# Moving the fourth RWKV batch behind four query tiles, with small group norm factors and attention second in the output projection

## The chip, the cores and the metric

The kernel runs on one core of one Trainium2 chip. The metric is the device time of one execution in microseconds (us). Engines: TensorE (PE, and PEld for its weight loads), VectorE (DVE), ScalarE (ACT), GpSimd (POOL) and SyncE (SP), which here only issues DMAs. Each engine takes its instructions in the order in which they were built and waits for others by semaphores.

## The reference

One layer of a hybrid decoder, for a prompt of 256 tokens and 8 single decode tokens, together T = 264 columns:

```python
x = x + 0.5 * swiglu(rmsnorm(x, n1), f1g, f1u, f1d)        # 2048 -> 5504 -> 2048
proj = rmsnorm(x, nm) @ w_in                                # 2048 -> 4864
o_att = attend(q, k, v, sinks)                              # 16 query heads, 4 kv heads, window 128
out, shift, S = rwkv_time_mix(...)                          # 16 heads of 64, a matrix state per head
x = x + concatenate([o_att, out]) @ w_out
x = x + 0.5 * swiglu(rmsnorm(x, n2), f2g, f2u, f2d)
y = rmsnorm(x, final_norm)
# in rwkv_time_mix, per head of 64:
mean = y.mean(-1); var = ((y - mean) ** 2).mean(-1)
yn = (y - mean) * rsqrt(var + GN_EPS) * ln_w + ln_b          # the group norm
out = (yn + bonus) * g
```

All numbers are float32, and the states, the key and value windows and the shifted columns are outputs too.

## The kernel before

Activations stand with features on the 128 partitions and the 264 tokens along the row. Every weight product (`gemm`, line 136) splits weights and activations into a high and a low part in float32r and adds three matmuls, hi·hi, hi·lo and lo·hi. A weight chunk (`chunk`, 125) is 128 rows by 4 blocks of 128: SyncE loads it into `raw` (6 buffers, line 131), ScalarE casts it to `hi` (132) and VectorE subtracts to get `lo` (133; 4 buffers each). So a chunk is twelve matmuls of 264 columns, and lines 131 to 133 run ahead of TensorE as far as the buffers allow. Results go to one of three `acc` buffers in PSUM; small products use five buffers named `m`.

Between the two feed-forward parts lies `mixing_body` (357). Its main loop walks `SEQ`, a written-out list: an entry `('b', i)` computes six tiles of `w_in` for two pairs of RWKV heads (batch i), `('kv', i)` one key or value tile, `('q', i)` one query tile. Side work is in generators, `tasks`: after each chunk `tick` (83) takes every task one `yield` further, and `pause(n)` sits out n ticks. `prep` (426) prepares a head pair; `chain` (553) does a batch's triangular solves (`X`, `Xt`, `st`, `PT`, `TT`), the state steps (`W`, `BT`, `N`, `S`) and the group norm (`gnorm`, 707); `attend` (760) handles a query tile and `dec_attend` (820) the decode tokens. After the loop the output projection runs in the three passes of `PASS`, each over some of the 16 input blocks (0 to 7 RWKV, 8 to 15 attention); `drain` first finishes the tasks that a pass needs. A scheduler then sets each engine's final order from modelled durations, with priority for lines 131 to 133.

Names: `pj` is a projected RWKV tile, `shc` its last columns (line 412), stored by ScalarE's DMA `out_sh` (887) once all 24 tiles are there; `o` is a query tile, `kv` a key tile, `y` a head pair's output, `gm` the masked products, `sa` their copy in DRAM, `XD` and `XR` the decode operands as they are and turned (701 to 704), `x` or `x0`, `x1` the residual, `e` and `s`, `dr` (new) a block for split activations, small factors and their copy in DRAM. Helper lines are named in the profile by the helper: 59 is `tt`, 62 `stt`, 69 `act`, 75 `mm`.

Of the kernel before, what the change touches and what calls it, by code (L numbers as in the profile page):

```python
# [24 lines left out]
HALF = (slice(0, 64), slice(64, 128))  # L25
# [5 lines left out]
ROW = 320  # L31
NWARM = 11
NGM, NKR, NUV, NTT, NBT = 10, 5, 3, 2, 5
NSTEP = 4
DWAIT = (11, 11, 11, 3)
PW = (2, 1, 3, 2, 9)
ALPHA = math.exp(-0.5)
LKV = 26
SEQ = [('b', 0), ('b', 1), ('b', 2), ('b', 3), ('kv', 0), ('kv', 1), ('kv', 2), ('kv', 3), ('q', 0), ('q', 1), ('q', 2), ('q', 3), ('q', 4), ('q', 5), ('q', 6), ('q', 7)]
PASS = [[0,1,2,3],[4,5,6,7],[8,9,10,11,12,13,14,15]]  # L40

VG1, VGM, VG2, VGF = 0, 16, 32, 48
VMU, VKK, VKA, VA0, VRK, VLW, VLB, VSK, VSD = 64, 90, 98, 106, 114, 122, 130, 138, 154
NVEC = 155
# [3 lines left out]
def body(tc, I, O):  # L48
    nc = tc.nc
    V, A, G, TE, SP = nc.vector, nc.scalar, nc.gpsimd, nc.tensor, nc.sync  # L50
# [3 lines left out]
    def uid(s):  # L54
        cnt[0] += 1
        return f"{s}{cnt[0]}"

    def tt(e, out, a, b, op):
        return e.tensor_tensor(out=out, in0=a, in1=b, op=op)  # L59
# [8 lines left out]
    def act(out, in_, f, **k):  # L68
        return A.activation(out=out, in_=in_, func=f, **k)  # L69

    def bc(ap, shape):
        return ap.broadcast_to(list(shape))

    def mm(out, lhsT, rhs, start=True, stop=True, **k):
        return TE.matmul(out, lhsT, rhs, start=start, stop=stop, **k)  # L75

    def behind(i):
        tc.add_manual_dep(i.ins, big[0].ins.name, mybir.DependencyInfo(mybir.DependencyClass.NoSync, mybir.DependencyReason.SCHED_ONLY))
        return i

    tasks = []

    def tick(hold=()):
        for g in list(tasks):
            if g not in hold and next(g, tasks) is tasks:
                tasks.remove(g)

# [12 lines left out]
    with ExitStack() as ctx:  # L100
# [56 lines left out]
        eps = cp.tile([P, 2], F32, name="eps")  # L157
# [199 lines left out]
        def mixing_body(mx, n2, n3, XD, XR):  # L357
# [3 lines left out]
            def ring(shape, tag, bufs):  # L361
                return mx.tile(list(shape), F32, tag=tag, bufs=bufs, name=uid(tag))
# [6 lines left out]
            ident, bo, cm = C[:, CID:CID + P], C[:, CBO:CBO + P], C[:, CCM:CCM + P]  # L369
# [50 lines left out]
            class Batch:  # L420
                pass

            def c4(x):
                return x[:, :NP].rearrange("p (c t) -> p c t", c=4)

# [127 lines left out]
            def chain(bt):  # L553
                n = bt.n
# [15 lines left out]
                for s in range(1, 31):  # L570
                    m, w = -(-s // ng), 31 - s
                    t = ring((ng * nr, m, w), "st", 2)
# [3 lines left out]
                    tt(V, Y[:, :m, s + 1:], Y[:, :m, s + 1:], t, ALU.add)  # L576
                    if s % NSTEP == 0:
                        yield
# [7 lines left out]
                for h in range(2):  # L586
                    x = h * 64
                    V.transpose(TT[x:x + 32, :, 0:32], TN[x:x + 32])
                yield from pause(7)
                ps = mp()  # L590
                for k in range(n):
                    for c in range(4):
                        for h in range(2):
                            j = k * 4 + c
# [3 lines left out]
                for h in range(2):  # L598
                    r = slice(h * 64 + 32, h * 64 + 64)
                    A.copy(zs[r], ps[r, :n * P].rearrange("p (c t) -> p c t", t=32))  # L600
                yield
                ps = mp()
                for j in range(4 * n):
                    for h in range(2):
                        r = slice(h * 64 + 32, h * 64 + 64)
                        mm(ps[h * 64:h * 64 + 32, j * 32:j * 32 + 32], zs[r, j, :], TT[r, j, 32:64])
                for h in range(2):
                    r = slice(h * 64, h * 64 + 32)
                    A.copy(TT[r, :, 32:64], ps[r, :n * P].rearrange("p (c t) -> p c t", t=32))
                yield  # L610
                Ys = [yb[bt.p0 + k] for k in range(n)]
                uv = bt.UV
                N = ring((P, n, 4, 64), "N", 1)
# [9 lines left out]
                for k in range(n):  # L623
                    v = wus[k].rearrange("p (c t) -> p c t", c=4)
                    for h in range(2):
                        (V.tensor_copy, A.copy)[h](uv[HALF[h], :, k, HALF[h]], v[HALF[h], :, 64:128])
                yield
                pbs = [mp() for _ in range(n)]
                for k in range(n):
                    for c in range(1, 4):  # L630
                        x = (c - 1) * P
                        for h in range(2):
                            r = HALF[h]
                            mm(pbs[k][r, x:x + 64], W[r, k, c - 1, :], bt.BT[k][r, c, r])
                        for h in range(2):
                            r = HALF[h]
# [23 lines left out]
                for c in range(1, 4):  # L660
                    ps = mp()
                    for k in range(n):
                        for h in range(2):
                            r = HALF[h]
                            mm(ps[r, k * 64:k * 64 + 64], PT[r, k, c - 1, :], S[r, k])
                    for k in range(n):
                        for h in range(2):
                            r = HALF[h]
# [13 lines left out]
                    A.dma_start(O["wkvp"][bt.p0 + k], S[:, k])  # L682
                g2s = [load(I["g2"][bt.p0 + k], (P, P)) for k in range(n)]
                gps = []
                gs = [gnorm(Ys[k]) for k in range(n)]
                for _ in range(PW[3] + 1):
                    for g in gs:
                        next(g)
                    yield
                for k in range(n):  # L690
                    p, o = bt.p0 + k, Ys[k]
# [3 lines left out]
                    stt(o, o, vc(VLB + p), gp[:, :T], ALU.add, ALU.mult)  # L695
                    mixed[p] = o
                if len(bts) == nbat and bt is bts[-1]:
                    ps = mp()
                    xt = mp()
                    for i in range(5):  # L700
                        TE.transpose((ps, xt)[i > 3][0:64, i % 4 * P:i % 4 * P + P], XD[:, i, :, :], ident)
                    for h in range(2):
                        A.copy(XR[HALF[h], 0:4], ps[0:64].rearrange("p (c t) -> p c t", c=4)[:, :, HALF[h]])
                        A.copy(XR[HALF[h], 4], xt[0:64, HALF[h]])
                yield

            def gnorm(y):
                yp = mp()
                mm(yp[:, :T], cm, y)
                r = tmp()  # L710
                act(r, yp[:, :T], AF.Square)
                yield from pause(PW[3])
                vp = mp()
                mm(vp[:, :T], bo, r)
                act(r, vp[:, :T], AF.Sqrt, scale=1.0 / 64, bias=eps[:, 1:2])
                V.reciprocal(r, r)
                tt(V, y, yp[:, :T], r, ALU.mult)
                yield
# [157 lines left out]
            bat, att, bts, scores = [], [], [], []  # L876
            for kind, i in SEQ:
                if kind == "b":
                    bt = newbatch(i)
                    for k in range(BATCH[i]):  # L880
                        p = bt.p0 + k
# [6 lines left out]
                elif kind == "kv":  # L888
                    w, p = i // 2, i % 2
                    ps = win(LKV + i)  # L890
# [12 lines left out]
                else:  # L903
                    ps = win(LKV + 4 + i)
                    q = ob[i]
# [21 lines left out]

            k0 = 0
            late = []
            n3.to = pairs(blk("y", 8, F32R))  # L930
            for pi, ks in enumerate(PASS):
                drain(need(ks))
                if ks[0] > 7:
                    late.append(blk("kv", 6, F32R))
                to = pairs(*(late + xs4[:2] if ks[0] > 7 else xs4[pi:pi + 1]))
                with tc.high_priority():
                    for k, t in zip(ks, to):
                        split(k, t)
                if ks[0] > 7:
                    drain(att)  # L940
                    with tc.high_priority():
                        for k in ks:
                            hi, lo = mixed[k]
                            src = odv[0][:, (k - 8) // 4, :, k % 4]
                            A.copy(hi[:, NP:], src)
                            tt((G, V)[k % 2], lo[:, NP:], src, hi[:, NP:].bitcast(F32), ALU.subtract)
                for o in range(KD):
                    ps = acc()
                    gemm(ps, I["wout"][o, :, k0 * P:(k0 + len(ks)) * P], [mixed[k] for k in ks], tick)
                    with tc.high_priority():  # L950
                        tt(V, xr[o], ps[:, :T], xr[o], ALU.add)
                    if pi == len(PASS) - 1 and o < CH:
                        n3.split(xr[o])
                for k in ks:
                    mixed[k] = None
                k0 += len(ks)
            n3.to += pairs(blk("o", 8, F32R), *late, *xs4[:2])
            return xr

        def second_ffn(n3, xr, XR):  # L960
# [153 lines left out]
```

## Time and profile before

| | |
|---|---|
| median of 3 runs | 1958.44 us (1957.58 to 1960.91) |
| the profiled execution | 1958.83 us, of which the span of its instructions is 1957.0 us |
| mean granted TensorE clock | 0.998 |
| PE, DVE, ACT busy share of the span | 99%, 67%, 53% |
| first feed-forward part, mixing, second feed-forward part | to about 757 us, to about 1205 us, to the end |

A row of the time line is: start in us, length, engine, line, operation, written tile <- read tiles, shapes, count, and in brackets how long the engine had been idle and what ended that. A row of the waits is: who waited <- for whom: us in total, times, longest. A row of a stage is: its limits, its length, and then the busy us (and instructions) of PE, PEld, DVE, ACT and POOL. A row of a group ends in busy us, mean ns of one | idle time before it. A row of a DMA ends in KB and median us from issue to landing.

### The profile page before, as it was taken

The page shows a single profiled execution, that of the slowest core. Times are in us where ns is not written, and L with a number is a line of the kernel's source. Part 1 is how long each engine was busy: PE and PEld are TensorE (multiplying, and loading weights), DVE is VectorE, ACT ScalarE, POOL GpSimd, SP SyncE. Part 2 cuts the span into 40 slices and gives each one's busy share as a digit, 9 for nine tenths or more (in the row PEclk, how much of TensorE's full clock was granted, in tenths as well). Part 3 has the DMA queues.
Part 4 walks back from the last instruction along what each step waited for, and adds up shares of the span by engine and source line. Part 5 has one row for each costly group of instructions (what it writes and reads, how often), then busy time and mean ns, then how long its engine had stood idle before and what let it go on. Part 6 is the DMA issues. An engine that isn't in the chain of part 4 may idle for free.

```text
span 1957.0 us, 45229 instructions
## 1 busy us (share of the span) xinstructions
PE 1940.1 (99%) x17011; PEld 1922.1 (98%) x17011; DVE 1313.1 (67%) x2591; ACT 1036.4 (53%) x2069; POOL 264.1 (13%) x382
## 2 busy tenths in 40 slices
PE   9999999999999999999999999999999999999998
PEld 9999999999999999999889999999999999999998
DVE  5865555655556567799988766766666666666665
ACT  5644444444444456665556755654444444444445
POOL 0401001010010122232210000210101001010012
PEclk9999999999999999999999999999999999999999
DMA  7666666666656567555455455566666666666654
GB/s 241 178 194 194 186 194 196 184 189 178 188 183 185 184 194 230 165 162 153 136 151 167 137 157 185 176 187 188 191 189 193 188 194 191 191 195 183 195 182 148
DMA packets 218875, 357.26 MB, mean 183 GB/s; under 512 B 33552, under 2 KB 72352, under 8 KB 218656
## 3 DMA queue, kind: packets, MB, share of 16 engines
q1 hardware_dynamic: 212144, 345.76, 59.4%
q10 hardware_dynamic: 6512, 8.61, 1.4%
q8 instruction: 133, 2.18, 0.4%
q14 instruction: 86, 0.70, 0.1%
HBM read 346.67 MB, written 9.69 MB: 182 GB/s over the span
## 4 chain that ended last, share of the span: by engine, by line
PE 95%; DVE 3%; DMA 1%; issue 1%; ACT 1%; SPq 0%; DVEq 0%; POOL 0%; ACTq 0%
PE acc L75 87%; PE m L75 7%; DVE lo L59 1%; DVE Xt L59 0%; DVE st L59 0%; DMA Xt<-sa 0%; DMA x<-in_x 0%; DMA raw<-in_win 0%; DVE y L59 0%; SPq L564 0%; DVE gm L59 0%; ACT t L69 0%; DMA sa<-gm 0%; PE m L782 0%; ACT BT L521 0%
## 5 line engine op out<-in xcount | busy, mean ns | idle before, releaser
L59 DVE TENSOR_TENSOR lo<-raw,hi 128x512 fp32r<-128x512 f32 (+1 forms) x1288 | 874.5, 683 | 511.0 <-ACT hi L132 489.8
L132 ACT CAST hi<-raw 128x512 fp32r<-128x512 f32 (+1 forms) x1288 | 777.0, 606 | 822.0 <-PE acc L75 741.5
L75 PE MATMUL acc<-x,hi 128*128 128x264 f32 x5034 | 932.7, 286 | 2.2 <-DVE o L62 1.2
L75 PEld LDWEIGHTS acc<-x,hi 128*128 128x128 f32 x5034 | 781.4, 189 | 5.8 <-ACT hi L132 2.4
L75 PE MATMUL acc<-x,lo 128*128 128x264 f32 x2517 | 719.8, 286 | 0.5 <-DVE lo L59 0.5
L75 PE MATMUL acc<-h,hi 128*128 128x264 f32 x2752 | 495.0, 284 | 0.0
L75 PEld LDWEIGHTS acc<-x,lo 128*128 128x128 f32 x2517 | 475.5, 189 | 2.9 <-DVE lo L59 1.3
L75 PEld LDWEIGHTS acc<-h,hi 128*128 128x128 f32 x2752 | 424.4, 189 | 0.0
L75 PE MATMUL acc<-h,lo 128*128 128x264 f32 x1376 | 387.8, 284 | 0.0
L75 PEld LDWEIGHTS acc<-h,lo 128*128 128x128 f32 x1376 | 259.2, 189 | 0.0
L59 POOL TENSOR_TENSOR t<-t,t 128x264 f32<-128x264 f32 x74 | 80.3, 1085 | 1095.9 <-DVE t L59 949.7
L75 PE MATMUL acc<-y,hi 128*128 128x264 f32 x648 | 122.7, 284 | 0.0
L75 PE MATMUL acc<-o,hi 128*128 128x264 f32 x648 | 120.1, 284 | 0.0
L75 PE MATMUL acc<-kv,hi 128*128 128x264 f32 x582 | 109.2, 284 | 0.0
L75 PEld LDWEIGHTS acc<-y,hi 128*128 128x128 f32 x648 | 101.2, 189 | 0.1
L75 PEld LDWEIGHTS acc<-o,hi 128*128 128x128 f32 x648 | 100.1, 189 | 0.0
L62 DVE SCALAR_TENSOR_TENSOR x<-acc,x 128x264 f32<-128x264 f32 x192 | 81.2, 427 | 24.5 <-PE acc L75 23.6
L75 PE MATMUL acc<-y,lo 128*128 128x264 f32 x324 | 92.0, 284 | 0.0
L75 PE MATMUL acc<-o,lo 128*128 128x264 f32 x324 | 92.0, 284 | 0.0
L75 PEld LDWEIGHTS acc<-kv,hi 128*128 128x128 f32 x582 | 90.0, 189 | 0.0
L59 DVE TENSOR_TENSOR t<-acc,t 128x264 f32<-128x264 f32 x156 | 67.4, 432 | 32.8 <-PE acc L75 32.8
L75 PE MATMUL acc<-kv,lo 128*128 128x264 f32 x291 | 82.7, 284 | 0.0
(280 smaller groups left out, 1534.9 us busy)
## 6 DMA issues: line engine op xcount, KB each, us to landing
raw<-in_gu SPq DMA_DIRECT2D x688, 256.0 KB, 3.4
raw<-in_dn SPq DMA_DIRECT2D x224, 256.0 KB, 2.9
raw<-in_win SPq DMA_DIRECT2D x152, 256.0 KB, 3.4
raw<-in_dn SPq DMA_DIRECT2D x160, 192.0 KB, 2.7
raw<-in_wout SPq DMA_DIRECT2D x64, 256.0 KB, 3.3
xsp<-x ACTq DMA_DIRECT2D x16, 132.0 KB, 3.6
x<-xsp SPq DMA_DIRECT2D x16, 132.0 KB, 4.0
ld<-in_sT SPq DMA_DIRECT2D x16, 128.0 KB, 3.7
```

What stands on the lines that cost most here:

```text
L59: return e.tensor_tensor(out=out, in0=a, in1=b, op=op)
L62: return V.scalar_tensor_tensor(out=out, in0=a, scalar=s, in1=b, op0=op0, op1=op1)
L75: return TE.matmul(out, lhsT, rhs, start=start, stop=stop, **k)
L132: A.copy(hi[:, :w], raw[:, :w])
```

## The change

Five things change. `SEQ` puts the fourth batch's tiles behind the key, value and first four query tiles. `PASS` takes the attention blocks second and blocks 4 to 7 last, with a new two-tile block `e` so that the attention pass does not take the first pass's block. For the first three batches the group norm's factors are computed once per token and head: three matmuls give the sums as 88 x 2 columns each, square root and reciprocal run on 88 x 6 numbers, and a DMA to DRAM and two DMAs back spread them over 64 partitions each; the centred `y` is kept in SBUF. The decode operands are turned by a task of their own, `turned`. Constant pauses get names.

```diff
+LAG = (7, 7, 7, 7)
+P1 = 1
+P2 = 1
+TURN = 3
+SMALL = (1, 1, 1, 0)
+HOP = (2, 3)
-SEQ = [('b', 0), ('b', 1), ('b', 2), ('b', 3), ('kv', 0), ..., ('kv', 3), ('q', 0), ..., ('q', 7)]
-PASS = [[0,1,2,3],[4,5,6,7],[8,9,10,11,12,13,14,15]]
+SEQ = [('b', 0), ('b', 1), ('b', 2), ('kv', 0), ..., ('kv', 3), ('q', 0), ..., ('q', 3), ('b', 3), ('q', 4), ..., ('q', 7)]
+PASS = [[0, 1, 2, 3], [8, 9, 10, 11, 12, 13, 14, 15], [4, 5, 6, 7]]
...
+            def sums(sq):
+                sm = mp()
+                for j in range(3):
+                    mm(sm[0:88, j * 2:j * 2 + 2], sq[:, j:T:3], bo[:, 0:P:64])
+                return sm[0:88, 0:6].rearrange("p (j h) -> p h j", h=2)
+
+            def spread(s, to):
+                d = dp.tile([2, T], F32, tag=uid("dr"), name=uid("dr"))
+                SP.dma_start(d.rearrange("h (p j) -> p h j", j=3), s)
+                yield from pause(HOP[0])
+                for h in range(2):
+                    behind(SP.dma_start(to[HALF[h]], bc(d[h:h + 1], (64, T))))
+                yield from pause(HOP[1])
...
-                yield from pause(7)
+                yield from pause(LAG[bt.i])
...
-                gs = [gnorm(Ys[k]) for k in range(n)]
-                for _ in range(PW[3] + 1):
+                gs = [gnorm(Ys[k], SMALL[bt.i]) for k in range(n)]
+                for _ in range(PW[3] + 1 + SMALL[bt.i] * sum(HOP)):
...
                 if len(bts) == nbat and bt is bts[-1]:
-                    ps = mp()
-                    xt = mp()
-                    for i in range(5):
-                        TE.transpose((ps, xt)[i > 3][0:64, i % 4 * P:i % 4 * P + P], XD[:, i, :, :], ident)
-                    for h in range(2):
-                        A.copy(XR[HALF[h], 0:4], ps[0:64].rearrange("p (c t) -> p c t", c=4)[:, :, HALF[h]])
-                        A.copy(XR[HALF[h], 4], xt[0:64, HALF[h]])
-                yield
-
-            def gnorm(y):
+                    spawn(turned())
+                yield
+
+            def turned():
+                yield from pause(TURN)
+                ps, xt = mp(), mp()
+                for i in range(5):
+                    TE.transpose((ps, xt)[i > 3][0:64, i % 4 * P:i % 4 * P + P], XD[:, i, :, :], ident)
+                yield
+                for h in range(2):
...
+            def gnorm(y, small):
                 yp = mp()
                 mm(yp[:, :T], cm, y)
                 r = tmp()
                 act(r, yp[:, :T], AF.Square)
+                if small:
+                    A.copy(y, yp[:, :T])
+                    yield from pause(PW[3])
+                    s = ring((88, 2, 3), "s", 4)
+                    act(s, sums(r), AF.Sqrt, scale=1.0 / 64, bias=eps[0:88, 1:2])
+                    V.reciprocal(s, s)
+                    yield from spread(s, r)
+                    tt(V, y, y, r, ALU.mult)
+                    yield
+                    return
...
+            more = blk("e", 2, F32R)
...
-                to = pairs(*(late + xs4[:2] if ks[0] > 7 else xs4[pi:pi + 1]))
+                to = pairs(*(late + [xs4[1], more] if ks[0] > 7 else xs4[:1]))
...
-            n3.to += pairs(blk("o", 8, F32R), *late, *xs4[:2])
+            drain(list(tasks))
+            n3.to += pairs(blk("o", 8, F32R), *late, xs4[1], more)
```

Three places where the order of instructions moves. The first is ScalarE around the store of `shc`; before, it stands in the second batch's chain (`TT` is that chain's tile):

```order
L600 COPY W_13184<-m_13497 32x256 x2
L132 CAST hi_14036<-raw_14035 128x512
L132 CAST hi_14077<-raw_14076 128x512
L887 DMA out_sh<-shc 128x234
L609 COPY TT_12420<-m_13534 32x8x32 x2
L132 CAST hi_14118<-raw_14117 128x512
```

Now, in the fourth batch's last tile (`t_15092` is that tile after the token shift):

```order
L74 ACTIVATE t_14983<-pj_10406,vec 128x256
L419 COPY t_14983<-ss 128x8
L419 COPY t_15092<-ss 128x8
L74 ACTIVATE t_15092<-pj_10407,vec 128x256
L920 DMA out_sh<-shc 128x234
L137 CAST hi_15331<-raw_15330 128x512
L137 CAST hi_15380<-raw_15379 128x512
```

The store moved from in front of the `TT` copies to behind the last tile's own activation, in front of weight casts.

The second is VectorE where the first query tile is read out of `acc` (`o_111<-acc`); before, with a value tile's evacuation (`t_14481<-acc_14262`) behind it:

```order
L580 STREAM_TRANSPOSE X_13454<-Xt_13455 128x256
L62 SCALAR_TENSOR_TENSOR o_111<-acc_14654,rs 128x264
L62 SCALAR_TENSOR_TENSOR t_14002<-t_13997,t_14002 128x264
L59 TENSOR_TENSOR lo_15055<-raw_15053,hi_15054 128x512
L59 TENSOR_TENSOR PT_14231<-X_13454,unit 128x256
L59 TENSOR_TENSOR bk_14147<-t_14002,t_14069 128x4x2x64
L59 TENSOR_TENSOR t_13997<-t_13997,t_13618 128x264
L585 STREAM_TRANSPOSE TT_13461<-PT_14231 128x8x32
L588 STREAM_TRANSPOSE TT_13461<-PT_14231 32x8x32 x2
L59 TENSOR_TENSOR lo_15083<-raw_15081,hi_15082 128x512
L62 SCALAR_TENSOR_TENSOR t_14106<-t_13434,vec,t_13997 128x264
L59 TENSOR_TENSOR t_14481<-acc_14262,rs 128x264
```

Now, where `t_13614<-acc_13457` reads out the last value tile:

```order
L599 STREAM_TRANSPOSE X_12413<-Xt_12414 128x256
L64 TENSOR_TENSOR PT_13205<-X_12413,unit 128x256
L604 STREAM_TRANSPOSE TT_12420<-PT_13205 128x8x32
L607 STREAM_TRANSPOSE TT_12420<-PT_13205 32x8x32 x2
L64 TENSOR_TENSOR t_12566<-m_13403,t_12566 128x8
L64 TENSOR_TENSOR t_13072<-m_13434,t_13072 128x8
L64 TENSOR_TENSOR t_13614<-acc_13457,rs 128x264
L64 TENSOR_TENSOR lo_13906<-raw_13904,hi_13905 128x512
L67 SCALAR_TENSOR_TENSOR o_111<-acc_13616,rs 128x264
```

The value tiles' evacuations moved from behind the first query tile's to ahead of it.

The third is VectorE in the third batch's group norm; before, with the reciprocals over 264 columns (L716) and the product that reads `m` in PSUM:

```order
L753 RECIPROCAL stb_14997<-stb_14997 128x4
L716 RECIPROCAL t_14928<-t_14928 128x264
L66 TENSOR_SCALAR t_14987<-t_14987,stb_14997 128x256
L66 TENSOR_SCALAR t_14988<-t_14988,stb_14997 128x128
L716 RECIPROCAL t_14932<-t_14932 128x264
L59 TENSOR_TENSOR lo_15893<-raw_15891,hi_15892 128x512
L62 SCALAR_TENSOR_TENSOR o_111<-acc_15634,rs 128x264
L59 TENSOR_TENSOR y_112<-m_14926,t_14928 128x264
```

Now, with the small reciprocals (L740), the preparation of the fourth batch's first head pair, and the product whose `t_14859` comes back from DRAM:

```order
L740 RECIPROCAL s_14925<-s_14925 88x6
L740 RECIPROCAL s_14934<-s_14934 88x6
L67 SCALAR_TENSOR_TENSOR kr_15008<-t_14885,t_14946 128x256
L64 TENSOR_TENSOR kr_15008<-t_14303,t_14946 128x256
L64 TENSOR_TENSOR lo_15122<-raw_15120,hi_15121 128x512
L64 TENSOR_TENSOR lo_15140<-raw_15138,hi_15139 128x512
L461 RECIPROCAL t_14886<-m_14943 128x264
L64 TENSOR_TENSOR pj_10406<-acc_14984,rs 128x264
L64 TENSOR_TENSOR y_112<-y_112,t_14859 128x264
L64 TENSOR_TENSOR lo_15158<-raw_15156,hi_15157 128x512
```

The two long reciprocals went, and between the small ones and the product stand other pairs' work and two weight chunks.

More of the change, by code (lines that the diff above doesn't have):

```diff
@@ L38 @@
 LKV = 26
-SEQ = [('b', 0), ('b', 1), ('b', 2), ('b', 3), ('kv', 0), ('kv', 1), ('kv', 2), ('kv', 3), ('q', 0), ('q', 1), ('q', 2), ('q', 3), ('q', 4), ('q', 5), ('q', 6), ('q', 7)]
-PASS = [[0,1,2,3],[4,5,6,7],[8,9,10,11,12,13,14,15]]
+SEQ = [('b', 0), ('b', 1), ('b', 2), ('kv', 0), ('kv', 1), ('kv', 2), ('kv', 3), ('q', 0), ('q', 1), ('q', 2), ('q', 3), ('b', 3), ('q', 4), ('q', 5), ('q', 6), ('q', 7)]
+PASS = [[0, 1, 2, 3], [8, 9, 10, 11, 12, 13, 14, 15], [4, 5, 6, 7]]
 VG1, VGM, VG2, VGF = 0, 16, 32, 48
@@ L609, in chain @@
                     A.copy(TT[r, :, 32:64], ps[r, :n * P].rearrange("p (c t) -> p c t", t=32))
-                yield
+                yield from pause(P1)
                 Ys = [yb[bt.p0 + k] for k in range(n)]
@@ L626, in chain @@
                         (V.tensor_copy, A.copy)[h](uv[HALF[h], :, k, HALF[h]], v[HALF[h], :, 64:128])
-                yield
+                yield from pause(P2)
                 pbs = [mp() for _ in range(n)]
@@ L697, in chain @@
                 if len(bts) == nbat and bt is bts[-1]:
-                    ps = mp()
-                    xt = mp()
-                    for i in range(5):
-                        TE.transpose((ps, xt)[i > 3][0:64, i % 4 * P:i % 4 * P + P], XD[:, i, :, :], ident)
-                    for h in range(2):
-                        A.copy(XR[HALF[h], 0:4], ps[0:64].rearrange("p (c t) -> p c t", c=4)[:, :, HALF[h]])
-                        A.copy(XR[HALF[h], 4], xt[0:64, HALF[h]])
-                yield
-            def gnorm(y):
+                    spawn(turned())
+                yield
+            def turned():
[5 more added lines that the diff above has]
+                for h in range(2):
+                    A.copy(XR[HALF[h], 0:4], ps[0:64].rearrange("p (c t) -> p c t", c=4)[:, :, HALF[h]])
+                    A.copy(XR[HALF[h], 4], xt[0:64, HALF[h]])
+            def gnorm(y, small):
                 yp = mp()
```

## Prediction

> **What bounds the kernel now.** I read the page's busy line, then busy time by stage, then the waits of TensorE, then the time line around each wait.
>
> ```profile
> PE 1940.1 (99%) x17011; PEld 1922.1 (98%) x17011; DVE 1313.1 (67%) x2591; ACT 1036.4 (53%) x2069; POOL 264.1 (13%) x382
> 65.80 691.23 PE acc L75 x5760
> 757.00:905.00 148.00, 147.10 (x1537) 142.79 (x1536) 123.52 (x290) 96.31 (x237) 39.26 (x98) 1.00 0.59 172
> 905.00:1050.00 145.00, 140.63 (x1623) 132.89 (x1622) 125.78 (x376) 86.12 (x212) 25.30 (x60) 1.00 0.51 141
> 1050.00:1150.00 100.00, 99.11 (x942) 94.46 (x941) 73.93 (x232) 67.09 (x195) 6.72 (x15) 1.00 0.54 156
> 1150.00:1205.00 55.00, 55.00 (x461) 55.00 (x460) 37.75 (x68) 28.46 (x54) 2.17 (x4) 1.00 0.59 181
> ```
>
> The second row is a piece of the chain of waits: 5760 weight matmuls in 691.23 us, 0.12 us each, so a chunk of twelve is 1.44 us. The four rows below it are busy times by stage (length, then PE, PEld, DVE, ACT, POOL; clock 1.00). TensorE is the bound everywhere. The change keeps every weight matmul, so it can only win TensorE's idle time: 0.9 us up to 905, 4.37 us to 1050, 0.89 us to 1150, none after. VectorE is 87% busy where most of it lies (125.78 of 145). TensorE's waits from 900 to 1150:
>
> ```profile
> PE m L75 <- ACT TT L609: 1.5, 1, 1.5
> PE m L75 <- DVE W L622: 1.3, 2, 0.9
> PE acc L75 <- DVE o L62: 1.2, 1, 1.2
> PE m L701 <- ACT XR L703: 0.4, 1, 0.4
> PE m L732 <- ACT XD L536: 0.3, 1, 0.3
> PE acc L75 <- DVE lo L59: 0.3, 1, 0.3
> PE acc L75 <- DVE x L59: 0.2, 1, 0.2
> ```
>
> Seven causes, 5.2 us in all. That is the purse; the idle 0.9 us before 905 lies where the instruction order does not change (the first difference on TensorE is the first batch's group norm, about 908 us).
>
> **The change part by part.** *The fourth batch behind four query tiles.* The longest wait:
>
> ```profile
> 950.62 0.19 DVE L59 TENSOR_TENSOR st<-X,Xt 128x30 f32<-128x30 f32 x1 [1.68 <-DMA Xt<-sa]
> 953.03 0.68 POOL L412 COPY shc<-pj 128x9 f32<-128x9 f32 x1 [4.38 <-DVE pj L59]
> 953.75 0.35 ACTq L887 DMA_DIRECT2D out_sh<-shc  x1
> 954.14 0.75 ACT L609 COPY TT<-m 32x256 f32<-32x256 f32 x2 [3.83 <-POOL shc L412]
> 954.55 1.15 PE L75 MATMUL m<-kr,TT 64*64 64x128 f32 x12 [1.46 <-ACT TT L609]
> ```
>
> VectorE stood 1.68 us for a DMA, so `pj` came late, GpSimd's `shc` copy after it, and ScalarE, whose queue held the `out_sh` store ahead of the `TT` copies, was idle 3.83 us. In the new ScalarE order (first place above) the store follows the last `pj`'s own activation and is followed by casts, not by `TT`. A wait there now delays casts. They run ahead of TensorE by up to the four `hi` buffers, three chunks or 4.3 us beside the one in use. I take the 1.46 us as gone, bounds 0 and 1.46. If that cover is gone, the same 3.83 us costs at most itself.
>
> The `o` wait:
>
> ```profile
> 991.68 1.80 DVE L442 RECIPROCAL t<-m 128x264 f32<-128x264 f32 x1
> 995.33 0.39 DVE L62 SCALAR_TENSOR_TENSOR o<-acc,rs 128x264 f32<-128x264 f32 x1
> 995.86 0.48 PE L75 MATMUL acc<-x,hi 128*128 128x264 f32 x2 [1.24 <-DVE o L62]
> ```
>
> Before, two value tiles still sat in `acc` buffers (their evacuations stand behind `o`, second place), so the second query tile needed the first one's buffer at once. Now both are read out ahead of `o`: 1.24 us gone.
>
> The two `W` waits: the later,
>
> ```profile
> 1023.48 0.22 DVE L59 TENSOR_TENSOR st<-X,Xt 128x72 f32<-128x72 f32 x1
> 1023.88 0.35 DVE L622 COPY W<-m 128x192 f32<-128x192 f32 x1
> 1024.28 0.33 PE L75 MATMUL m<-BT,W 64*64 64x64 f32 x4 [0.89 <-DVE W L622]
> ```
>
> comes from a triangular solve's `st`/`Xt` pairs mixed in front of the `W` copy. In the new order only weight `lo`s and one `uv` copy stand there for the second and third batch. Gone, 1.3 us for both. The `XD` wait (0.3 us) has the same neighbours as before; it stays.
>
> *Small group norm factors, batches one to three.*
>
> ```profile
> L442 DVE RECIPROCAL t<-m 128x264 f32<-128x264 f32 x8 | 14.4, 1801 | 0.9 <-PE m L75 0.9
> L716 DVE RECIPROCAL t<-t 128x264 f32<-128x264 f32 x8 | 14.3, 1795 | 3.0 <-ACT t L69 3.0
> 1043.25 0.61 PE L75 MATMUL m<-t,C 128*128 128x264 f32 x2
> 1043.50 0.48 PE L75 MATMUL acc<-x,lo 128*128 128x264 f32 x1
> 1043.82 0.41 PE L75 MATMUL acc<-x,hi 128*128 128x264 f32 x2
> 1946.13 0.54 PEld L75 LDWEIGHTS m<-ones,sq 128*88 128x88 f32 x6 [0.73 <-ACT sq L69]
> 1946.60 0.75 PEld L75 LDWEIGHTS m<-sq,ones 128*128 128x128 f32 x6
> 1947.09 0.17 DVE L991 RECIPROCAL rt<-rt 88x3 f32<-88x3 f32 x1 [1.53 <-ACT rt L69]
> ```
>
> Six reciprocals of 1.80 us become six of about 0.17 us (row L991, 88x3 for 88x6): VectorE is freed of 6 x 1.63 = 9.8 us. That ends the `lo` wait of 0.3 us, which two such reciprocals precede. On TensorE one 264-column product, 1043.25 to 1043.82 less the 0.12 us of one weight matmul, 0.45 us, is replaced by three of 88 columns of weights and a two-column stream. The nearest rows are the six loads of 88 columns, 1946.13 to 1946.60, 0.47 us: +0.02 each, six times +0.1 us. The reads with a step of three are not in the trace; the dearer bound is the six 128-column loads, 0.75 us, +1.8 us in all; the lower bound is 0. I take +0.1, the row of the same width. ScalarE copies six times 264 columns where it took their square root: even, and it is not the bound.
>
> The wait that this adds: VectorE's product `y<-y,t` now waits for a write to DRAM and two reads issued on SyncE.
>
> ```profile
> sa<-gm SPq DMA_DIRECT2D x32, 16.0 KB, 1.7
> Xt<-sa SPq DMA_DIRECT2D x16, 32.0 KB, 2.9
> L59 DVE TENSOR_TENSOR lo<-raw,hi 128x512 fp32r<-128x512 f32 (+1 forms) x1288 | 874.5, 683 | 511.0 <-ACT hi L132 489.8
> L62 DVE SCALAR_TENSOR_TENSOR x<-acc,x 128x264 f32<-128x264 f32 x192 | 81.2, 427 | 24.5 <-PE acc L75 23.6
> SPq L131 <- DVE lo L59: 914.7, 946, 4.0
> ```
>
> The write is 1.7 us by the row and the read 2.9 us; an issue takes 0.35 us (the store at 953.75), so the second half, with a weight load before it, goes out 0.7 us after the first: an estimated 5.3 us. In the third batch (third place) VectorE does a 0.17 us reciprocal, two `kr` and a `pj` of about 0.43, two `lo` of 0.68 and a 1.80 us reciprocal in between: 4.6 us. So it stands about 0.7 us, and behind it stand `lo`s, which TensorE needs up to three chunks (4.3 us) later. Cost 0; without that cover 0.7 us a batch. The Trainium skill ("DMA: Bandwidth & Descriptors", Anatomy of one DMA) puts a fixed cost of about 2.0 us on each DMA, mostly the write receipt, worst towards HBM: two in series 4.0 us plus the issues, and the sum would be the same. SyncE holds weight loads behind the two waits on the write, some 2 us; the last row shows that it waits for buffers, 914.7 us in 946 waits, so its loads are early by far more than that.
>
> *Attention second, [4..7] last.* Same 768 matmuls. The last pass has 1.44 us per output tile, VectorE 0.68 + 0.43 = 1.11 us and for the first four tiles a norm split of about 0.43 more, 0.1 us over: covered by the chunks ahead, 0.4 us otherwise. Attention's pass begins 24 weight matmuls (2.9 us) after the last attention product instead of 37 (4.4 us):
>
> ```profile
> 1149.96 0.38 PE L75 MATMUL m<-t,kv 128*128 128x128 f32 x2
> 1151.17 0.97 POOL L59 TENSOR_TENSOR kv<-o,kv 128x256 fp32r<-128x256 f32 x1 [2.00 <-ACT kv L921]
> 1152.61 0.73 POOL L59 TENSOR_TENSOR kv<-o,kv 128x256 fp32r<-128x256 f32 x1
> ```
>
> GpSimd's last `kv` split ended 1153.34, 3.0 us after that product; its tile is used 0.7 us into the pass. Margin 0.6 us: cost 0, at worst 0.5 us.
>
> *The rest.* `turned` as a task: the fifth transpose no longer stands behind its copy (XR, 0.4 us, and the `x` wait right behind it, 0.2 us): gone, 0.6 us. `LAG`, `P1`, `P2` equal the old pauses; block `e` only changes an address; the final drain comes after the last pass, with nothing left in it: 0.
>
> **The sum.** Gone: 1.46 + 1.24 + 1.3 + 0.3 + 0.6 = 4.9 of 5.26 us. But the new order was also laid out to have no waits, as the old one was, and real durations will make some. I charge the rate of the stage where VectorE has the load that it will have: 199.71 us in 245 less 9.8 is 78%, near the 74% of 1050 to 1150, which idles 0.89 per 100 us. Over 245 us: 2.2 us left. Change: -5.26 + 2.2 + 0.1 = -3.0. The profiled execution took 1958.83 (span 1957.0 and 1.83 around it), 0.39 above the median: 1955.8, or **1955.5 us** as a median.
>
> **Rivals.** (1) *All idle time goes*: -5.26 + 0: 1953.2. For it, the named causes nearly fill the purse; against it, no stage with this much small work is free of idle. Chance 0.17. (2) *Waits only move*: the stage of the second and third chain now has key and query tiles beside it, just as the third and fourth had, and idles 4.37 again: 1958.4, up to 1960 with the dearer loads. For it, that stretch has most of the waits; against, the orders differ at each named place. Chance 0.22. (3) *The hop holds VectorE*: the one DMA-gated wait followed above, 1.68 us on VectorE, became 1.46 us on TensorE. Six new gated products, each passing on as much, cost 8.8 us; with 4.9 won and 0.1 paid, +4.0: 1962.5. It decides where the round trip is over 4.6 + 4.3 = 8.9 us, or where `lo` has lost its lead. For it, the write is 176 runs of 12 bytes, which no row shows; against, 128-byte runs take 1.7 us. The skill's page (Specifications) says that below 512 bytes the engine reads, modifies and writes; `sa` is below it too. Chance 0.10. (4) *The moved tiles give nothing* because ScalarE's store stalls casts: the 1.46 stays, 1957. Chance 0.03. My forecast, a change of -1.5 to -4.5 us, has 0.48.
>
> **How the numbers follow.** A measurement tells about 0.2%, 3.9 us, from no change: under 1954.5 is faster, over 1962.4 slower. Faster: all of (1) and 0.13 of the forecast: 0.30. Slower: (3) and a little of (2)'s far end, less the part of (3) under the bound: 0.09. Same: 0.61. The range, 1953.0 to 1960.0, takes in (1), (2) with the dearer loads and leaves out (3).
>
> **What would show it.** Right: TensorE idle 905 to 1150 about 2 us, no wait on `TT` behind a store, none on `o`, `XR`; VectorE's reciprocals at the norm near 0.17 us. Wrong: VectorE idle on a DMA `t<-dr` for over 4 us with TensorE waiting on `lo`; six `88x2` groups over 0.7 us each; TensorE waiting on `kv` at the attention pass; or waits of 4 us at new places.

## The result and the profile after

The changed kernel takes 1970.84 us (median of 4, 1970.35 to 1971.32) where the kernel before took 1959.68 (median of 4): ratio 1.0057, 95% interval 1.0045 to 1.0069. It is 11.2 us slower; 1955.5 was predicted, 1953 to 1960 as the range. The profiled span grew from 1957.0 to 1968.9 us.

TensorE's waits from 860 to 1215 us in the changed kernel (waits of both stages; the sum, the count, the longest):

```profile
PE m L80 <- DMA ld<-in_kc: 4.3, 1, 4.3
PE acc L80 <- DVE lo L64: 3.1, 3, 2.7
PE m L80 <- DVE t L819: 1.7, 1, 1.7
PE m L80 <- DVE PT L64: 1.1, 1, 1.1
PE m L80 <- ACT BT L540: 0.4, 1, 0.4
PE m L80 <- ACT t L818: 0.2, 1, 0.2
```

Of the waits listed in the prediction (`TT`, `W`, `o`, `XR`, `XD`, `x`, `lo`) only `lo` is left, and longer; the `PT` wait was there before, ahead of the change. New ones took their place. By stage (the first two rows answer to the two stages shown before), and then around the two longest waits, cut where the clock changes:

```profile
905.00:1050.00 145.00, 139.96 (x1520) 132.61 (x1519) 105.62 (x336) 88.17 (x232) 14.90 (x46) 0.99 0.48 131
1050.00:1150.00 100.00, 95.30 (x999) 90.57 (x997) 77.17 (x252) 58.93 (x173) 15.10 (x32) 0.98 0.57 165
...
922.00:925.12 3.12, 0.52 (x5) 0.30 (x3) 3.06 (x8) 0.49 (x1) 0.70 (x2) 1.00 0.39 121
925.12:928.54 3.42, 3.29 (x15) 3.29 (x16) 3.39 (x10) 1.97 (x4) 0.78 (x2) 0.50 0.50 136
...
1088.00:1099.20 11.20, 6.94 (x59) 6.70 (x58) 9.35 (x43) 7.85 (x28) 0.76 (x1) 1.00 0.93 289
1099.20:1102.62 3.42, 3.42 (x16) 3.27 (x15) 1.76 (x6) 0.83 (x2) 0.00 (x0) 0.50 0.68 208
```

VectorE was relieved (105.62 us for 125.78 in the first of these stages): the reciprocals took 9.7 us less, as planned, and 6.9 us came back in the two stages behind, with work of the fourth batch. TensorE still idles 9.74 us in the two stages where it idled 5.26. Behind each of the two long waits stands a stretch of 3.42 us at clock 0.50 with 15 or 16 matmuls. The page before has no such stretch ahead of its last 8 us.

**The first long wait** is the small factors' copy. SyncE, then VectorE, then TensorE on the time line of the changed kernel:

```profile
909.83 0.33 SPq L136 DMA_DIRECT2D raw<-in_win  x1
910.87 0.76 SPq L436 DMA_DIRECT2D dr<-s  x2
911.73 0.37 SPq L371 DMA_DIRECT2D ld<-in_sT  x1
914.89 2.41 SPq L439 DMA_DIRECT2D t<-dr  x2
917.41 0.54 SPq L136 DMA_DIRECT2D raw<-in_win  x1
...
911.12 0.18 DVE L740 RECIPROCAL s<-s 88x6 f32<-88x6 f32 x1
919.43 0.43 DVE L64 TENSOR_TENSOR y<-y,t 128x264 f32<-128x264 f32 x1 [3.25 <-DMA t<-dr]
...
925.25 0.59 PE L80 MATMUL acc<-x,lo 128*128 128x264 f32 x1 [2.73 <-DVE lo L64]
```

From the first copy's issue (910.87) to the product 8.6 us pass, not 5.3. SyncE waits for the writes to land before it can issue the reads (its row in the waits from 905 to 1150 us is below), and issues no weight load for 7.6 us (909.83 to 917.41), time for five chunks. VectorE stands for 3.25 us, and the `lo`s behind it come late. The second batch's copy does the same: VectorE stands for 3.04 us, and the copy (line 819) that TensorE waits for, the third row of its waits above, is behind that product.

```profile
SPq L439 <- DMA dr<-s: 6.6, 3, 2.7
...
987.25 0.43 DVE L64 TENSOR_TENSOR y<-y,t 128x264 f32<-128x264 f32 x1 [3.04 <-DMA t<-dr]
988.05 0.28 DVE L819 COPY t<-m 128x128 f32<-128x128 f32 x1
988.39 0.81 PE L80 MATMUL m<-t,kv 128*128 128x256 f32 x3 [1.69 <-DVE t L819]
```

In the third batch VectorE stands for 1.03 us (at 1042 us), with two `lo` waits of 0.2 us behind it.

**The second** is on SyncE alone:

```profile
1081.62 0.86 SPq L371 DMA_DIRECT2D ld<-in_kc  x2
1082.56 1.82 SPq L949 DMA_DIRECT2D x<-xsp  x4
...
1090.80 2.38 SPq L949 DMA_DIRECT2D x<-xsp  x4
1093.28 0.38 SPq L136 DMA_DIRECT2D raw<-in_wout  x1
1093.70 0.90 SPq L371 DMA_DIRECT2D ld<-in_kc  x2
...
1098.19 1.06 PE L80 MATMUL m<-qb,ld 128*128 128x8 f32 x8 [4.26 <-DMA ld<-in_kc]
```

The last two loads of decode keys stand behind all sixteen reloads of the residual (`x<-xsp`), 11 us of issuing; TensorE reached their matmuls at 1093.9.

**Two costs without a wait.** The small sums, and block `e` in the second feed-forward part:

```profile
1032.31 1.50 PE L80 MATMUL m<-C,t 128*88 128x2 f32 x12
1033.67 0.37 PE L80 MATMUL acc<-x,lo 128*128 128x264 f32 x1
1033.88 0.40 PE L80 MATMUL acc<-x,hi 128*128 128x264 f32 x2
...
1402.16 0.40 PE L80 MATMUL acc<-e,hi 128*128 128x264 f32 x2
...
1403.26 0.40 PE L80 MATMUL acc<-y,hi 128*128 128x264 f32 x2
```

Twelve records for two pairs last from 1032.31 to 1033.88 less one weight matmul, 1.45 us, 0.73 a pair; the product before cost 0.45. That is +0.27 for each of six pairs, 1.65 us. From the first matmul of `e` to the third tile of `y` nine start within 1.10 us, where nine others take 1.08 (0.120 each). It is 0.02 us in every tile of the gate and up products; from the first matmul of `e` there to the first of its last tile 669.43 us pass, where 667.88 do in e_pad below, which differs only in the place of `e`: 1.55 us.

The account: waits +4.5 (9.74 less 5.26), half clock +3.4 (half of 3.29 and 3.42 us), sums +1.65, block `e` +1.55: 11.1 of the 11.9 us by which the span grew. I have not placed the last 0.8. Of the waits, 4.26 us are the keys' and 4.8 those behind the copies (2.73, 1.69 and 0.4).

### The profile page after: what moved, and what is told of

Read it like the earlier page. It is cut to its first block, busy times and chain, and to the rows that moved or that the text cites. A ratio compares the mean times of both kernels' runs of the same rounds, so it can differ in the third digit from the quotient of the medians.

```text
span 1968.9 us, 45335 instructions
## 1 busy us (share of the span) xinstructions
PE 1948.2 (99%) x17035; PEld 1930.0 (98%) x17035; DVE 1306.9 (66%) x2591; ACT 1034.9 (53%) x2073; POOL 261.6 (13%) x382
## 4 chain that ended last, share of the span: by engine, by line
PE 94%; DMA 2%; DVE 2%; ACT 1%; issue 0%; SPq 0%; DVEq 0%; POOL 0%; ACTq 0%; POOLq 0%
PE acc L80 86%; PE m L80 7%; ACT t L74 1%; DVE lo L64 0%; DMA t<-dr 0%; DVE y L64 0%; DMA ld<-in_bias 0%; DMA x<-xsp 0%; DMA ld<-in_kc 0%; DMA dr<-s 0%; ACT L74 0%; DMA raw<-in_wout 0%; DVE t L808 0%; DMA raw<-in_win 0%; DMA ld<-in_sT 0%
## 5 line engine op out<-in xcount | busy, mean ns | idle before, releaser
L80 PE MATMUL acc<-x,hi 128*128 128x264 f32 x4840 | 897.6, 286 | 0.0
L80 PEld LDWEIGHTS acc<-x,hi 128*128 128x128 f32 x4840 | 753.1, 190 | 2.8 <-ACT hi L137 0.3
L80 PE MATMUL acc<-x,lo 128*128 128x264 f32 x2420 | 692.5, 287 | 3.1 <-DVE lo L64 3.1
L80 PEld LDWEIGHTS acc<-x,lo 128*128 128x128 f32 x2420 | 458.6, 190 | 5.6 <-DVE lo L64 4.2
```

## The experiments

Each edit is on the changed kernel unless it says otherwise; ratios are to the kernel before, whose median was 1959.1 to 1960.4 us beside them.

**e_pad.** `blk`: `(16 if tag == "y" else 0)` becomes `(16 if tag == "e" else 0)`.

> The changed kernel with one edit: the 16 spare columns that end block y end block e instead, so that block e starts 64 bytes earlier in SBUF and the addresses of everything behind it stay. In the changed kernel each chunk set of the second feed-forward part that reads block e takes some 22 ns longer: matmuls on e and on the tiles behind it start 122 to 128 ns apart instead of 120. Address theory: e's place makes these matmuls slower; every start in the second part is 120 ns apart again, and the time falls by 1.5 us, to about 1969.3. Rival (the order of the blocks, or what else runs then): the 122 to 128 ns stay and the time stays at 1970.8.

1969.44 us, 1.4 less; ratio 1.0053 (1.0038 to 1.0068). The same nine matmuls on its time line:

```profile
1402.34 0.40 PE L80 MATMUL acc<-e,hi 128*128 128x264 f32 x2
...
1403.42 0.28 PE L80 MATMUL acc<-y,hi 128*128 128x264 f32 x1
```

1.08 us, and no excess is left in the whole second part. The address is the cause: in the built program at its old place `e` lies 32 bytes past a multiple of 128, as the weight tiles do, and the other blocks that these products stream 96 past; with the edit `e` is at 96 too, and nothing else moves. It is the trace that shows it: the interval of this ratio overlaps the changed kernel's.

**e_xsp.**

```diff
-            for o in range(KD):
+            for o in range(4):
                 SP.dma_start(xr[o], xsp[o])
...
+                    if not pi and o + 4 < KD:
+                        SP.dma_start(xr[o + 4], xsp[o + 4])
                     ps = acc()
```

> The changed kernel with one edit: of the sixteen reloads of the residual that stood in one block on SyncE ahead of the first pass of the output projection, twelve are issued one by one during that pass, so that the last two loads of decode keys stand behind eight reloads instead of sixteen. Queue theory: TensorE's longest wait (4.26 us, for these keys, at 1098 us) is SyncE's issuing of the reloads ahead of them; some 5 us earlier the keys are there, the wait goes, and with it the stretch of half-speed matmuls behind it (about 1.5 to 2 us): the time falls by 5.5 to 6.5 us, to 1964.5 to 1965.5. If the half-speed stretch doesn't come from the wait, it falls by 4.3, to 1966.5. Rival (waits only move): TensorE then waits for something else near 1100 us, and the time falls by less than 2 us.

1962.69 us, 8.2 less; ratio 1.0020 (1.0011 to 1.0030). The wait on the keys is gone, and the first `lo` wait shrank (waits of the same stretch, all of them):

```profile
PE acc L80 <- DVE lo L64: 2.3, 3, 1.8
PE m L80 <- DVE PT L64: 1.4, 2, 1.0
PE m L80 <- DVE t L819: 1.1, 1, 1.1
PE m L80 <- ACT BT L540: 0.4, 1, 0.4
```

Waits fell by 5.4 us, and both half-clock stretches (3.4 us) are gone. It brought more than expected because the first `lo` wait was shorter and left the clock alone in this profile; why it was shorter is not shown.

**e_big.** `SMALL = (0, 0, 0, 0)`. **e_all:** this with the two edits above.

> The changed kernel with the old group norm factors for every batch (SMALL all 0): no sums on 88 rows, no copy to DRAM and back. Hop theory: the first batch's round trip stops VectorE for 3.25 us at 916 us, raw loads stand behind it on SyncE, and TensorE's wait of 2.73 us at 925 us with the half-speed matmuls behind it (about 1.4 us) comes from that; the 88x2 sums take TensorE some 0.27 us each more than the 264-column ones did, 1.6 us for six. All that goes: 5 to 6 us less, 1965 to 1966. Rival (order theory: what costs is the place of the batches and the attention, and the six factors were a gain on VectorE, 1.46 us each): the wait at 925 us stays or comes back behind VectorE's longer work, and the time stays within 1.5 us of 1970.8 or rises.

> The changed kernel with the three edits above together: block e 64 bytes earlier, the reloads spread over the first pass, and the old group norm factors everywhere; what is left of the change is the fourth batch's place, the attention second in the output projection and the turning as a task. Sum theory (three separate prices): 1970.8 less 1.5, 6 and 5.5 is 1957.8, within 2 us of the kernel before. Rival (waits move): above 1962. Should the moves alone bring what the prediction gave them (4.9 us of waits gone, 2.2 charged), it would come out at 1956 to 1957.

1979.96 us (ratio 1.0105, 1.0090 to 1.0120) and 1978.58 (1.0099, 1.0084 to 1.0114). Here my hop theory fell: without the copies the kernel is 9 us slower still, and the sum theory missed with it. The waits at 925 and 988 us are indeed gone, but (waits of e_big, the first three of its list, and the stage of the attention's end):

```profile
PE m L876 <- DVE t L71: 3.1, 1, 3.1
PE m L815 <- DVE t L64: 1.6, 1, 1.6
PE m L80 <- ACT BT L540: 1.5, 1, 1.5
...
1050.00:1150.00 100.00, 90.42 (x891) 83.56 (x890) 76.26 (x250) 58.45 (x177) 16.12 (x35) 0.93 0.48 144
```

9.6 us idle and a clock of 0.93 in one stage: by VectorE's time line the fourth batch's solves and the last softmaxes fall together on VectorE ahead of the attention pass. In the new order the short reciprocals are a gain, and the order itself is the dear part; no run parts the place of the batch from the place of the attention pass. It also shows that e_xsp's gain is not a fixed price: e_all has this edit and e_pad's, and is only 1.4 us below e_big.

**e_small**: the old `SEQ`, `PASS` and blocks, small factors on. **e_turn**: the same with `SMALL` off, so only the turning is new.

> The small factors and the turning task alone: the changed kernel with SEQ, PASS and the blocks of the passes as in the kernel before. Order theory (the fourth batch's place and the attention as second pass cost most of the loss): with the old order the time comes within 3 us of the kernel before; TensorE still pays for the six sums (two pairs take 1.36 us for twelve matmul records in the changed kernel where the 264-column ones took 0.25 us a pair, so 0.43 us a pair, 2.6 us in all), so 1960 to 1962. Hop theory (the copy to DRAM and back costs most): 1964 to 1968, with VectorE idle for 3 us on the copy and TensorE waiting on lo behind it. If the sums were nearly free, as the prediction had it, 1956 to 1958.

> Nothing but the turning as a task of its own: the changed kernel with the old SEQ, PASS and blocks and the old group norm factors. The kernel before waits 0.62 us at 1101 us for the turned operands and the residual sum behind them. Either theory: 0.6 us less than the kernel before at best, 1958.5 to 1959.5 beside a kernel before of 1959.1; with the wait only moved, the same as before.

1962.13 us (1.0016, 1.0007 to 1.0026): about as the order theory had it, but with 5.0 us of `lo` waits in its profile (of an execution of 1965.32 us). 1961.99 us (1.0016, 1.0007 to 1.0026) for the turning alone: a miss, it was to be no slower. Its waits are as long as before; but its profile has three stretches at half clock, here two of them with what lies beside the first:

```profile
1077.00:1084.19 7.19, 7.19 (x78) 6.64 (x77) 4.13 (x19) 3.74 (x15) 0.49 (x2) 1.00 0.46 134
1084.19:1087.60 3.41, 3.41 (x29) 3.04 (x28) 2.10 (x8) 2.17 (x8) 0.00 (x0) 0.50 0.56 179
...
1145.63:1149.04 3.41, 3.41 (x18) 3.23 (x16) 0.29 (x1) 0.68 (x2) 0.00 (x0) 0.50 0.35 111
```

TensorE never idles there: it runs small products (8-column scores, 64x64 states). The kernel before, which runs such products at nearly the same times, kept its clock in its profile. Its other runs differ in this: of the 25 beside e_turn, 15 have a mean clock of 0.998 and take 1957.8 to 1960.4 us, five have 0.996 and take 1959.6 to 1962.1. Only one of e_turn's ten has 0.998, and it takes 1959.2. Nor is the turning shown to bring the stretches: e_sh below, which does not have it, has two at nearly the same places (1011.46 and 1083.14 us; e_turn's first is at 1012.51).

**e_idle2, e_idle4** measure the clock by itself: the kernel before with five waits in the second feed-forward part (e_idle4 with the reciprocal twice).

```diff
+                    if not begin and pi and f == f0 + 3:
+                        w8 = tmp()
+                        with tc.high_priority():
+                            V.reciprocal(w8, pgu[1][:, :T])
+                            held[0] = mm(mp()[:, :8], ones, w8[:, :8])
                     pgu = [acc(), acc()]
```

> The kernel before with five waits put into its second feed-forward part, one in each of the last five parts of the gate and up products: a reciprocal on VectorE of the last product (1.8 us) and a matmul on its result ahead of the next chunk, so that TensorE idles some 2 to 2.4 us each time; nothing is left out of the outputs. Clock theory: a wait costs itself, and only a long one costs a stretch at half clock behind it; the waits of 1.7 and 1.8 us seen in the changed kernels had none, those of 2.7 and 4.3 us had one of 3.4 us. Then five waits cost 10 to 12 us and the clock's record shows no stretch at 0.5. Rival (every wait costs one): 5 x (2.2 + 1.7) = 19 us, with five stretches.

> The same with two reciprocals in a row, so that TensorE idles some 4 to 4.2 us at each of the five places. Clock theory: each is followed (or crossed) by one or two stretches of 3.4 us at half clock, worth about 1.7 us of matmuls each: 5 x (4.1 + 1.7 to 3.4) = 29 to 37 us over the kernel before. Rival (the half-clock stretches have nothing to do with the waits): 5 x 4.1 = 20 to 21 us, and no stretch at 0.5 in the second part.

1976.00 us (ratio 1.0080, 1.0062 to 1.0098) and 2000.75 (1.0206, 1.0188 to 1.0225). The waits of each, and stretches behind one wait of e_idle2 and two of e_idle4:

```profile
PE m L75 <- DVE t L264: 11.5, 5, 2.3
1500.78:1504.19 3.41, 3.41 (x17) 3.41 (x17) 0.69 (x1) 0.79 (x2) 0.00 (x0) 0.50 0.36 94
```

```profile
PE m L75 <- DVE t L265: 24.9, 5, 5.0
1380.95:1387.78 6.83, 5.64 (x25) 5.64 (x26) 3.62 (x7) 0.62 (x1) 0.00 (x0) 0.50 0.19 59
1510.66:1517.48 6.82, 6.32 (x29) 6.32 (x29) 1.14 (x2) 1.04 (x2) 0.00 (x0) 0.50 0.19 50
```

Five waits of 2.3 us: two had a stretch behind them, three none. Five of 5.0 us (longer than I had put it): all five, four of them twice as long. Both expectations were partly wrong: length alone does not decide below 3.4 us. e_xp below has a `lo` wait of 2.97 us and no stretch ahead of its end, e_pad one of 2.28 us with a stretch behind it. The costs add up: 11.5 and two times 1.7 is 14.9 of the 15.7 us by which e_idle2's span grew. In e_idle4 the five waits are 24.9 us and the matmuls that run at half clock behind them lose 13, 38 of 41.9; one more stretch, at 1084 us, is worth 1.7.

**e_xphop**: both mends of e_pad and e_xsp, and `HOP = (4, 6)`. **e_xps0**: both, and `SMALL = (0, 1, 1, 0)`. **e_xppool**: both, and `spread` issues its three DMAs by `G` instead of `SP`.

> The changed kernel with block e 64 bytes earlier, the reloads spread over the first pass, and longer pauses around the copy of the small factors (HOP 4 and 6 chunks instead of 2 and 3). Hop theory: the read from DRAM no longer holds SyncE and the product no longer holds VectorE at 916 us; TensorE's wait of 1.8 to 2.7 us at 925 us goes: 1958 to 1959.5, where the two edits without it would give 1961.2 (1962.7 less 1.5). Order theory: the five longer ticks push the batches' chains later and the waits come back elsewhere, above all at the attention pass: 1961 or more.

> The changed kernel with block e 64 bytes earlier, the reloads spread, and the old group norm factors for the first batch only. Hop theory: the first batch's wait at 925 us goes (1.8 us with the reloads spread) and two of the six sums (0.9 us), so 2 to 3 us less than the 1961.2 of the two edits: 1958 to 1959.5. Order theory: VectorE's two 1.8 us reciprocals are back beside the key tiles, waits come back there, and the time stays at 1961 or more.

> The changed kernel with block e 64 bytes earlier, the reloads spread, and the small factors' copy to DRAM and back issued by GpSimd instead of SyncE, so that no load of weights stands behind a wait for it. Hop theory with SyncE as the one held: the wait of 1.8 us on lo at 924 us goes: 1959 to 1960. With VectorE as the one held (its product waits 3.3 us for the copy): the wait stays and the time is the 1961.2 of the two edits. Should GpSimd's issuing be slower, the waits grow: 1962 or more.

1972.24 us (1.0065, 1.0050 to 1.0080), 1964.18 (1.0022, 1.0012 to 1.0032) and 1968.79 (1.0044, 1.0031 to 1.0058): no way of easing the copy helps (e_xp below is both mends alone, 1962.01). With the longer pauses VectorE still stands 3.0 us for the copy and TensorE 2.3 for `lo`, and 3.8 us are new behind the softmax at 1092. Without the first batch's copy VectorE's waits for copies fall to 0.8 us and the `lo` wait is gone, but 3.9 us are new at 1084. On GpSimd a read takes 4.6 us to land (3.0 on SyncE); the first batch's copy holds VectorE for only 0.29 us there and the `lo` wait at 925 us is gone, as the theory with SyncE as the one held had it, but 9 us of waits are spread over ten places and the time that it gave (1959 to 1960) was missed.

**e_sh**: the kernel before with the store of `shc` behind the first query tile; no other instruction moves.

> The kernel before with one edit: ScalarE's store of the shifted columns is issued behind the first query tile instead of ahead of the second batch's TT copy; no other instruction changes its place. The kernel before waits 1.46 us on that copy at 954 us, which stands on ScalarE behind the store. Queue theory: the wait goes and nothing takes its place: 1.4 us less, ratio 0.9993. Rival (waits move): the copies wait for something else, or a later wait grows, and the time is the same within 0.5 us.

1959.86 us, ratio 0.9999 (0.9990 to 1.0008). The `TT` wait of 1.46 us is gone, the `W` wait 4.6 us later grew from 0.38 to 1.51, and the later `W` wait of 0.89 is gone: 1.2 us less of waits, where the profile has two half-clock stretches that the profile before lacks. The ratio expected, 0.9993, lies inside the interval, so the time cannot tell a small gain from none.

**e_xp**: the two mends alone. **e_f32r**: with them, squares and ones of the small sums in float32r. **e_f32r1**: this with `SMALL = (0, 0, 1, 0)`.

> The changed kernel with its two mends that proved themselves one at a time: block e 64 bytes earlier and the reloads spread over the first pass. Sum theory: 1962.7 less the 1.4 of the block is 1961.3, ratio to the kernel before 1.0009 to 1.0014; the trace keeps the six sums (2.6 us dearer than the kernel before's) and TensorE's waits of some 5 us, as many as before. Rival (waits move with every edit): 1963 or more.

> The same with the squares and the ones of the small sums rounded to float32r, so that each of the three sums of a pair is one matmul record instead of two; this rounds the squares that go into the group norm's variance. Price theory (what is left of the loss is TensorE's time for the sums, 0.68 us a pair against 0.25): half of 4.1 us goes for the six pairs, 1.9 to 2.1 us less than without it, 1959.3, as fast as the kernel before. Hop theory (what is left is the waits around the copy): 1961 or more.

> The same with small factors for the third batch only. Price and hop theories both give less: two copies and four sums fewer, 1958.5 to 1959.5. Rival (order theory: the six short reciprocals are what makes room for the fourth batch's solves on VectorE; without them the waits come back as with none): 1962 or more, with waits behind VectorE near 1085 us.

1962.01 us (1.0009, 1.0000 to 1.0018), as the sum theory had it: the two mends take the loss from 11.2 to 1.8 us. 1964.36 (1.0020, 1.0011 to 1.0029) and 1967.49 (1.0031, 1.0019 to 1.0043): misses of the price theory. e_f32r1 is where its order rival put it, with waits of 1.9 us behind ScalarE and 2.1 behind VectorE at 1088 and 1092. In e_f32r the sums did become cheap (three records from 1033.19 to 1033.46, 0.35 us a pair with what follows, so 2.2 us less in six), but TensorE's waits from 860 to 1215 us rose from 6.9 to 10.6 us; the longest new ones:

```profile
PE acc L80 <- DVE x L64: 3.1, 1, 3.1
...
PE m L80 <- ACT BT L543: 2.2, 1, 2.2
```

The time of the sums is real, and yet no price that could be taken off here: with the shorter instructions the waits came at other places. No version of the change beats the kernel before.

## Why the prediction was wrong

- *Which waits go* was nearly right: `TT`, `o`, both `W`, `XR` and `x` are gone, and `XD` too, which was to stay. That each is worth its length is not shown: e_sh took `TT` away, another wait grew, and no gain could be measured.
- *The charge for new waits*, 2.2 us from the next stage's rate, was the step that failed first: 9.7 us came. A rate of idle time has no single wait in it, and three single waits (2.7, 1.7 and 4.3 us) make 8.7 of these.
- *The hop* was put at 5.3 us and took 8.6 in the first batch and 9.2 in the second (issued at 978.05). In the first the reads left 4.0 us after the copies' issue, where 1.7 for the write was reckoned. SyncE issued no weight load for 7.6 us, where some 2 were reckoned; that TensorE waited for a load is not shown, as the last cast before its wait ended at 919.55 and the `lo` that it waited for began at 924.50, on VectorE. The cover was worked out for the third batch; in the first two VectorE stood for 3.25 and 3.04 us and TensorE for 2.73 and 1.69, so "cost 0" failed. This is the third rival's mechanism, in two batches of three, at about the 8.9 us that it named. The Trainium skill's fixed cost of about 2.0 us for a DMA ("DMA: Bandwidth & Descriptors", Anatomy of one DMA, which measures those that GpSimd issues), as an estimate 4.0 for two in series, is less than half of the 8.6.
- *The attention pass* was judged by GpSimd's `kv` split alone, and no wait on `kv` came. But the decode keys' loads, which the moved query tiles bring with them, were not followed past the sixteen reloads on SyncE: 4.3 us, shown by e_xsp.
- *Small sums*, +0.02 us each, cost +0.27; the dearer bound (1.8 for six) held with 1.65.
- *Block `e`, "only changes an address: 0"*, cost 1.55 us, shown by e_pad's trace.
- *The clock* was in no term: 3.4 us behind the two long waits.
- *The turning*, -0.6, is not shown to win anything: alone it was 2.4 us slower, at a lower clock; whether it lowers the clock is open.

What decides whether VectorE's 9.8 us help was only partly seen: under the old order small factors bring nothing (e_small and e_turn, 1962.1 and 1962.0), under the new one they save 9 us (e_big).

Two of the signs that it named for being wrong came: sums over 0.7 us a pair, and a wait of 4 us at a new place.

## What to carry over

Where a change moves a task, follow each of its loads through the issuing queue and ask what block of transfers now stands ahead of it: that was the longest wait here, and a few lines mended it. Beside a TensorE wait of 2 us or more allow for a stretch at half clock (here worth nothing, or 1.7 to 3.2 us), and do not count a wait as won until the next one on the same chain has been looked at. A new tile is placed at an address; look whether the blocks behind and beside it keep theirs.

## What the hardware showed

- The granted clock goes to 0.50 for 3.41 us or a multiple of it, on a grid: in e_idle4 the stretches begin at 1380.95, 1510.66 and 1640.37 us, each 129.71 us or 38 times 3.413 apart. The Trainium skill ("TensorE: Matmul & The Clock Gate", Part 1) describes a free-running window of 3413 ns and half rate after at least one idle window; the 5.0 us waits agree (four of them fill a step of the grid, the other all but 0.25 us of one). Two of five 2.3 us waits and e_turn's stretches without any wait do not: less than an idle window was enough. What decides is open. In e_idle2 the two waits with a stretch put 1.9 us into one step of the grid, the other three at most 1.3; but e_xp's first `lo` wait put 1.9 into one step and had none, e_pad's 1.6 and had one.
- Matmuls that stream an activation block which lies 32 bytes past a multiple of 128, as the weights do, and the first ones behind them, start up to 129 ns apart instead of 120. Only this one move of 64 bytes was tried, so the rule behind it is open.
- A float32 matmul record with 88 columns of weights and a two-column stream takes 0.11 us (1.36 us for twelve, 1032.31 to 1033.67), nearly as long as a weight matmul of 264 columns (0.12).
